# One transformer block on one core: Up's block products 512 wide with partial sums kept in one PSUM bank, and two of four weight sums added in DRAM by transfers during the input projection

## The chip, the core and the metric

The kernel runs on one core of one Trainium2 chip. Its engines, as the profile names them, are PE (matrix products), PEld (PE's weight loads), DVE, ACT and POOL (elementwise work), and SP, which here only issues transfers. All transfers, from whichever engine they are issued, go through the core's 16 DMA engines. Partial sums of products lie in PSUM, in banks of 128 x 512 float32; everything else that is worked on lies in SBUF; weights and intermediates that don't fit lie in DRAM.

The metric is the device time of one execution in microseconds, as the median of several runs. Times inside an execution come from one profiled execution, counted from the start of its span.

## The reference

One layer over 512 tokens of width 2048, in float32:

```python
xn = _rmsnorm(h, norm_mix[l]); y = xn @ w_in[l]
o_gdn = _gdn_group(y[..., :GDN_COLS], ...)      # 8 heads x 128
o_rwkv = _rwkv_group(y[..., GDN_COLS:], ...)    # 16 heads x 64
h = h + concat([o_gdn, o_rwkv]) @ w_out[l]
h = h + _cross_attention(_rmsnorm(h, ...), _rmsnorm(mem, ...), ...)   # 256 memory tokens
hn = _rmsnorm(h, norm_mlp[l])
h = h + jnp.square(jax.nn.relu(hn @ mlp_w_up[l])) @ mlp_w_down[l]     # hidden width 8192
return _rmsnorm(h, norm_final)
```

The line that the change rewrites is `hn @ mlp_w_up`, called Up: 512 x 2048 by 2048 x 8192.

## The kernel before

**Precision.** Each float32 operand of a large product is split into two parts, hi (rounded to a type that PE reads at full rate) and lo (what is left). `split` (L128) does it with one cast on ACT (L130) and one subtraction on DVE (L131). A product is hi x hi + hi x lo + lo x hi, three matmuls through `mm` (L121, L122) into one PSUM bank.

**Stages.** In order of time: the input projection (instructions named py) together with the recurrent heads, up to about 943 us; the projections kp, kq, vp, vo for the cross attention; op (the product with w_out), sc and at (the attention itself); Up from 1688 to 2336 us; Down (dn) from 2336 to 3044 us; the final norm.

**The projection stage** is recorded as chains of instructions and put in order by a list scheduler (`issue` L243, `run` L275), so all its instructions carry the line L247. It keeps a model clock for each engine and issues the chain whose next instruction can start first, with a rank to settle ties. `projections` (L523) is the chain of the large products; one chain each does a group of RWKV heads and a GDN head. Each of these inverts small triangular matrices in `inverse_blocks` (L717): the blocks go to DRAM (nd), come back in another layout (sr or sgi), POOL works through 30 small operations on them, and the result goes out again (bg16T, bg16U, bg8T, bg8U) and comes back to SBUF as r and E (RWKV) or gk and gqn (GDN), from where PE's matmuls ri and gi use it. All these transfers are issued by SP, in program order.

**Up** (L1406 to L1549) is a Strassen scheme in Winograd's form. The hidden columns are 32 blocks of 256; for each block p the 2048 x 256 weights are four quarters a11, a12, a21, a22, each laid out as 128 x 1024 (8 slices of 128 x 128), and the activations four halves of tokens and rows. Seven products, B11, T1, T2, T3, T4, B22 and B21, take the place of eight. Their activation sides are made once, by `place` (L1393) and `put` (L1385), into `comb[i][k]`: a tile of 128 x 512 whose half HA is hi and whose half HB is lo, for each product i and each of 8 slices k. Their weight sides are four sums per block (s1, s2, a21, s4), added on DVE (L1438). `product` (L1421) splits its weights and issues 24 matmuls of 256 columns, here the first 16:

```python
for z, k in enumerate(ks):
    sl = slice(z * P, z * P + P)
    mm(pt, hi[:, sl], comb[i][k][:, HA], start=z == 0, stop=False)
    mm(pt, hi[:, sl], comb[i][k][:, HB], start=False, stop=False)
```

and then 8 of lo with HA, all into the first 256 columns of one bank. Each product has a bank of its own until it is read: the copy of B11 to SBUF on ACT (L1456), and seven additions of 256 columns on DVE that put the four result quarters together (c11, c12 in c1, c21, c22 in c2). `square` (L1535) then applies the norm's scale and the squared ReLU in pieces of 256 columns (DVE L1537, ACT L1538) and stores the block to DRAM (Ud, from ACT, L1540). Block 0 uses another order of products, with B21 and T4 right behind B11, since the norm's scale rstd is made meanwhile (`used`, L1542).

**Buffers and queues.** Weights come in by SP, 512 KB each, four for each block, into three buffers of the tag wraw (NWR) and three of wraw2; split parts have two buffers each (NWS). PSUM tags mx, mg and mm have two banks each. An engine works through its instructions in order, and a semaphore wait holds up all that is queued behind it.

Of the kernel before, what the change touches and what calls it, by code (L numbers as in the profile page):

```python
# [73 lines left out]
def build(tc, I, out):  # L74
# [168 lines left out]
    def issue(op):  # L243
        eng, nm, f, a, k, out, ins, slack = op
        t = start(op)
        d = cost(op)
        f(*a, **k)  # L247
        if eng == "SP":
            clock[eng] = t + 330
            size = math.prod(out.shape) * 4  # L250
            state["dma"] = max(state["dma"], t + 330) + size / 300
            t, eng = max(state["dma"] + 700, t + 2900) + slack[1], "DMA"
        else:
            t += d
            clock[eng] = t
        if eng == "PE":
            state["shape"] = None if ins[0].dtype == F32R else (ins[0].partition_size(), ins[0].free_size())
        if eng == "ACT" and len(a) > 2 and a[2] in (AF.Tanh, AF.Ln, AF.Exp):
# [83 lines left out]
    VOd = [pd.tile([P, 8, 512], F32, name=f"vod{i}", tag=f"vod{i}") for i in range(4)]  # L342

# [852 lines left out]

    issue(pieceload(0))
# [18 lines left out]
    chain(projections(), 4)  # L1216
    chain(rwkv(0), 3)
# [167 lines left out]
    def put(i, k, src):  # L1385
        t = comb[i][k]
        S.copy(t[:, HA], src)
        V.tensor_tensor(out=t[:, HB], in0=src, in1=t[:, HA].bitcast(F32), op=ALU.subtract)
# [4 lines left out]
    def place(i, k, e, o):  # L1393
# [6 lines left out]
        elif i == T3:  # L1400
            sub(e[:, HB], o[:, HB], e[:, HB])
        elif i == T4:
            sub(e[:, HA], e[:, HA], o[:, HA])
        put(i, k, o[:, HB] if i == B22 else o[:, HA] if i == B21 else e[:, HB] if i == T3 else e[:, HA])

    def strassen(nm, pool, src, ks, done, used=None, first=False):  # L1406
# [4 lines left out]
        w = len(ks) * P  # L1411

        def raw(p_, tag, bufs, i):
            cnt[0] += 1
            r = p_.tile([P, 1024], F32, tag=tag, name=f"{tag}_{cnt[0]}", bufs=bufs)[:, 0:w] \
                if p_ is pw else p_.tile([P, pool[1]], F32, tag=tag, name=f"{tag}_{cnt[0]}", bufs=bufs)[:, 0:w]
            if i is not None:
                nc.sync.dma_start(r, src[i])
            return r

        def product(i, tag, a):  # L1421
            cnt[0] += 1
# [12 lines left out]
            return pt  # L1435

        def add(o, a, b, op=ALU.add):
            V.tensor_tensor(out=o, in0=a, in1=b, op=op)  # L1438
# [17 lines left out]
        S.copy(u1, p1)  # L1456
# [250 lines left out]
```

## Time and profile before

| | us |
|---|---|
| median of 3 runs (3055.92 to 3060.02) | 3057.31 |
| span of the profiled execution | 3053.3 |
| median less span | 4.0 |
| PE busy, of the span | 3022.5 |
| DVE busy | 1916.1 |
| ACT busy | 1355.4 |
| POOL busy | 216.3 |
| bytes moved by the core's transfers | 403.14 MB |

PE is the engine to watch: it is busy for all but 31 us of the span. In the views below, "busy" of an engine counts its instructions' time; an idle time in square brackets stands before an instruction and names what ended it; a row of the chain or of the timeline has the start, the length, the engine, line and operation, then output<-inputs, and xN for N equal instructions run together. A line number is that of the kernel before. The page's window figures list the busy time of PE, PEld, DVE, ACT and POOL with their instruction counts, PE's granted clock, the share of the DMA engines' time and the GB/s moved.

### The profile page before, as it was taken

To read this page: it belongs to the slowest core of one execution; us is meant where nothing else is said; L and a number is where in the kernel's file an instruction comes from. 1 tells how busy PE (TensorE), PEld (TensorE's weight loads), DVE (VectorE), ACT (ScalarE), POOL (GpSimd) and SP (SyncE) were. 2 spreads that over 40 slices of the span, in tenths; PEclk is the share of its full clock that TensorE was granted. 3 is DMA by queue.
4 is the path that set the end of the run, shared out by engine and by line. 5 is a ranking of instruction groups with operands and counts; after the bars stand their busy time and mean duration, and the time that the engine had idled before them with its cause. 6 is when DMAs were issued, how large, how long until landed. Compare 5 with 4: busy or idle time off the path is not lost.

```text
span 3053.3 us, 50831 instructions
## 1 busy us (share of the span) xinstructions
PE 3022.5 (99%) x20740; PEld 2607.5 (85%) x20740; DVE 1916.1 (63%) x2881; ACT 1355.4 (44%) x1864; POOL 216.3 (7%) x547
## 2 busy tenths in 40 slices
PE   9999999999999999999999999999999999999998
PEld 7888878878878898778878999999999888888887
DVE  7666666666677647534348888888887443444457
ACT  6455455455555555533336544444444222222234
POOL 0312311312312000000000000000000000000000
PEclk9999999999999999999999999999999999999999
DMA  5322322323425586753323433333334332333335
GB/s 186 104 80 80 108 80 80 108 80 87 135 73 162 172 272 231 262 201 122 110 92 90 142 130 130 132 132 135 125 135 163 124 118 104 125 125 125 113 130 180
DMA packets 226746, 403.14 MB, mean 132 GB/s; under 512 B 91656, under 2 KB 115468, under 8 KB 226512
## 3 DMA queue, kind: packets, MB, share of 16 engines
q1 hardware_dynamic: 210384, 372.62, 37.5%
q10 hardware_dynamic: 16128, 27.27, 2.4%
q8 instruction: 163, 2.67, 0.3%
q14 instruction: 71, 0.58, 0.1%
HBM read 352.23 MB, written 47.59 MB: 131 GB/s over the span
## 4 chain that ended last, share of the span: by engine, by line
PE 95%; DVE 1%; ACT 1%; DMA 1%; issue 1%; POOL 0%; SPq 0%; DVEq 0%; ACTq 0%; POOLq 0%
PE dn L122 23%; PE up L122 21%; PE py L247 21%; PE op L122 6%; PE vp L122 3%; PE sc L122 3%; PE at L122 3%; PE kq L247 3%; PE vo L122 3%; PE kp L247 2%; PE rs L247 1%; PE gs L247 1%; PE pgB L247 1%; PE po L247 0%; PE gpo L247 0%
## 5 line engine op out<-in xcount | busy, mean ns | idle before, releaser
L130 ACT CAST whi<-wraw 128x1024 fp32r<-128x1024 f32 x384 | 403.6, 1051 | 814.3 <-PE dn L122 474.8
L131 DVE TENSOR_TENSOR wlo<-wraw,whi 128x1024 fp32r<-128x1024 f32 x384 | 469.7, 1223 | 135.6 <-ACT whi L130 131.5
L122 PE MATMUL up<-cb,whi 128*128 128x256 f32 x3584 | 467.4, 283 | 1.3 <-ACT whi L130 0.7
L122 PEld LDWEIGHTS up<-cb,whi 128*128 128x128 f32 x3584 | 446.3, 192 | 2.4 <-ACT whi L130 1.7
L122 PE MATMUL dn<-ul,whi 128*128 128x512 f32 (+1 forms) x1032 | 395.0, 389 | 0.9 <-ACT whi L130 0.9
L122 PE MATMUL dn<-uh,whi 128*128 128x512 f32 x1024 | 393.8, 390 | 0.0
L122 PE MATMUL dn<-uh,wlo 128*128 128x512 f32 (+1 forms) x1024 | 384.5, 375 | 0.0
L247 PE MATMUL py<-xhi,whi 128*128 128x512 f32 x928 | 371.8, 401 | 6.1 <-ACT xhi L247 6.0
L247 PE MATMUL py<-xhi,wlo 128*128 128x512 f32 x928 | 371.7, 401 | 0.0
L247 PE MATMUL py<-xlo,whi 128*128 128x512 f32 x928 | 371.4, 400 | 0.3 <-DVE xlo L247 0.3
L247 DVE TENSOR_TENSOR wlo<-wraw,whi 128x1024 fp32r<-128x1024 f32 (+1 forms) x180 | 221.7, 1231 | 128.2 <-ACT whi L247 126.5
L1559 DVE TENSOR_TENSOR h<-h,dn 128x512 f32<-128x512 f32 x112 | 77.0, 688 | 331.1 <-PE dn L122 331.1
L247 ACT CAST whi<-wraw 128x1024 fp32r<-128x1024 f32 (+1 forms) x180 | 188.2, 1046 | 203.0 <-PE py L247 165.3
L122 PE MATMUL up<-cb,wlo 128*128 128x256 f32 x1792 | 251.5, 283 | 0.0
L122 PEld LDWEIGHTS up<-cb,wlo 128*128 128x128 f32 x1792 | 231.2, 192 | 0.0
L122 PEld LDWEIGHTS dn<-ul,whi 128*128 128x128 f32 x1032 | 193.9, 188 | 41.2 <-ACT whi L130 1.2
L122 PEld LDWEIGHTS dn<-uh,whi 128*128 128x128 f32 x1024 | 192.2, 188 | 40.9
L122 PEld LDWEIGHTS dn<-uh,wlo 128*128 128x128 f32 x1024 | 192.3, 188 | 35.0
L247 PEld LDWEIGHTS py<-xhi,whi 128*128 128x128 f32 x928 | 174.9, 188 | 41.2 <-ACT xhi L247 6.2
L247 PEld LDWEIGHTS py<-xlo,whi 128*128 128x128 f32 x928 | 174.9, 188 | 35.6 <-DVE xlo L247 1.4
L247 PEld LDWEIGHTS py<-xhi,wlo 128*128 128x128 f32 x928 | 174.9, 189 | 35.3 <-issue 1.0
L130 ACT CAST whi<-ws 128x1024 fp32r<-128x1024 f32 x96 | 100.5, 1047 | 150.8 <-PE up L122 93.9
(741 smaller groups left out, 5145.4 us busy)
## 6 DMA issues: line engine op xcount, KB each, us to landing
wraw<-in_w_dn SPq DMA_DIRECT2D x144, 512.0 KB, 3.5
wraw<-in_w_up SPq DMA_DIRECT2D x128, 512.0 KB, 3.5
wraw<-in_w_in SPq DMA_DIRECT2D x116, 512.0 KB, 3.6
wraw<-in_wk SPq DMA_DIRECT2D x32, 512.0 KB, 3.9
wraw<-in_wqT SPq DMA_DIRECT2D x32, 512.0 KB, 5.4
wraw<-in_wv SPq DMA_DIRECT2D x32, 512.0 KB, 4.6
wraw<-in_wo SPq DMA_DIRECT2D x32, 512.0 KB, 5.9
wraw<-in_w_out SPq DMA_DIRECT2D x32, 512.0 KB, 3.9
```

Source lines behind the costliest of these rows:

```text
L122: PE.matmul(o, l, r, start=start, stop=stop)
L130: S.copy(hi, src)
L131: V.tensor_tensor(out=lo, in0=src, in1=hi.bitcast(F32), op=ALU.subtract)
L247: f(*a, **k)
L1559: V.tensor_tensor(out=hres[n], in0=hres[n], in1=pt, op=ALU.add)
```

## The change

Three things are changed.

**Wider products.** In `product`, hi meets the whole tile `comb[i][k]`, HA and HB at once: one matmul of 512 columns into a whole bank instead of two of 256 into one half of it. The bank's first half then holds hi x hi (to which 8 matmuls of lo x hi are added), its second half hi x lo. A product is 16 matmuls. Whoever reads a product adds the two halves: `both` copies the second half on ACT and adds the first on DVE; other readers add twice on DVE.

**Accumulating products.** The seven products use three banks, x, y and z. B11, T2, T3 and T4 go one after the other into x, without clearing it, T1 and B22 into y, B21 into z; the running sum is read out in between. So the sums of results are made partly by PE's accumulation. Every block has the order B11, T1, T2, B21, T3, B22, T4. Some signs are turned (B11 and B22 negated, and with them c1's, so that `square` takes the minimum there), and `square` works at the full width of 512.

**Two sums in DRAM.** Of the four weight sums, a21 + a22 and a11 + a21 are made ahead of Up by a new chain, `background`, in the projection stage: at each third step of py, ACT issues two copies of 1 MB from w_up to new arrays in DRAM, and POOL, one step later, two transfers that add another 1 MB of w_up onto them. There are 17 such steps, 32 copies and 32 accumulating transfers. Up then loads the finished sums: five loads of 512 KB for each block instead of four, into three buffers of one kind and five of the other. Two sums stay on DVE. The weights' layout pairs two blocks, so that a row of 8 KB holds both.

```diff
-        d = cost(op)
+        move = nm == "dma_start" and eng != "SP"
+        d = 100.0 if move else cost(op)
...
+    def background():
+
+        for u in range(17):
+            yield after("py", 3 * u + 4)
+            if u < 16:
+                for i, b in ((0, 2), (1, 0)):
+                    yield AC.dma_start(SUMS[i][u], I["w_up"][u, b])
+            if u > 0:
+                for i in (0, 1):
+                    yield GS.dma_start(SUMS[i][u - 1], I["w_up"][u - 1, 1], accum_op=ALU.add, max_dma_last_dim=2048)
...
-    def put(i, k, src):
+    def put(i, k, src, neg=False):
         t = comb[i][k]
-        S.copy(t[:, HA], src)
-        V.tensor_tensor(out=t[:, HB], in0=src, in1=t[:, HA].bitcast(F32), op=ALU.subtract)
+        split(src, t[:, HA], t[:, HB], -1.0 if neg else None)
 
     def sub(o, a, b):
         V.tensor_tensor(out=o, in0=a, in1=b, op=ALU.subtract)
@@ -1398,95 +1414,73 @@
         elif i == T2:
             sub(e[:, HA], o[:, HB], e[:, HA])
         elif i == T3:
-            sub(e[:, HB], o[:, HB], e[:, HB])
+            sub(e[:, HB], e[:, HB], o[:, HB])
         elif i == T4:
-            sub(e[:, HA], e[:, HA], o[:, HA])
-        put(i, k, o[:, HB] if i == B22 else o[:, HA] if i == B21 else e[:, HB] if i == T3 else e[:, HA])
-
-    def strassen(nm, pool, src, ks, done, used=None, first=False):
-
-
-
-
-        w = len(ks) * P
-
-        def raw(p_, tag, bufs, i):
+            sub(e[:, HA], o[:, HA], e[:, HA])
+        put(i, k, o[:, HB] if i == B22 else o[:, HA] if i == B21 else e[:, HB] if i == T3 else e[:, HA],
+            i in (B11, B22))
...
+        def raw(src):
+            i = nraw[0] % 8
+            nraw[0] += 1
+            r = pw.tile([P, 1024], F32, tag="wraw", name=f"ua{nraw[0]}", bufs=NWR) if i % 3 == 0 else \
+                pool.tile([P, 1024], F32, tag="wraw2", name=f"ub{nraw[0]}", bufs=5)
+            nc.sync.dma_start(r, src[:, p % 2 * 1024:p % 2 * 1024 + 1024])
+            return r
+
+        def product(i, pt, a, start=True):
             cnt[0] += 1
-            r = p_.tile([P, 1024], F32, tag=tag, name=f"{tag}_{cnt[0]}", bufs=bufs)[:, 0:w] \
-                if p_ is pw else p_.tile([P, pool[1]], F32, tag=tag, name=f"{tag}_{cnt[0]}", bufs=bufs)[:, 0:w]
-            if i is not None:
-                nc.sync.dma_start(r, src[i])
-            return r
-
-        def product(i, tag, a):
-            cnt[0] += 1
-            hi = pw.tile([P, 1024], F32R, tag="whi", name=f"whi{cnt[0]}", bufs=NWS)[:, 0:w]
-            lo = pw.tile([P, 1024], F32R, tag="wlo", name=f"wlo{cnt[0]}", bufs=NWS)[:, 0:w]
+            hi = pw.tile([P, 1024], F32R, tag="whi", name=f"whi{cnt[0]}", bufs=NWS)
+            lo = pw.tile([P, 1024], F32R, tag="wlo", name=f"wlo{cnt[0]}", bufs=NWS)
             split(a, hi, lo)
-            pt = psb(f"{nm}_{i}", tag)[:, 0:M]
-            for z, k in enumerate(ks):
-                sl = slice(z * P, z * P + P)
-                mm(pt, hi[:, sl], comb[i][k][:, HA], start=z == 0, stop=False)
-                mm(pt, hi[:, sl], comb[i][k][:, HB], start=False, stop=False)
-            for z, k in enumerate(ks):
-                mm(pt, lo[:, z * P:z * P + P], comb[i][k][:, HA], start=False, stop=z == len(ks) - 1)
+            for k in range(8):
+                PE.matmul(pt, hi[:, k * P:k * P + P], comb[i][k], start=start and k == 0, stop=False, skip_group_check=True)
+            for k in range(8):
+                PE.matmul(pt[:, HA], lo[:, k * P:k * P + P], comb[i][k][:, HA], start=False, stop=k == 7, skip_group_check=True)
             if used:
                 used(i)
-            return pt
-
-        def add(o, a, b, op=ALU.add):
+
+        def tt(o, a, b, op=ALU.add):
             V.tensor_tensor(out=o, in0=a, in1=b, op=op)
 
-        def wraw2(i):
-            return raw(pool[0], "wraw2", 3, i)
-
-        def ws():
-            return raw(pool[0], "ws", 2, None)
-
-        a11 = raw(pw, "wraw", NWR, 0)
-        if first:
-            a12, a22 = raw(pw, "wraw", NWR, 3), raw(pw, "wraw", NWR, 2)
-            a21 = wraw2(1)
-        else:
-            a21 = raw(pw, "wraw", NWR, 1)
-            a22, a12 = wraw2(2), wraw2(3)
-        p1 = product(B11, "mx", a11)
-        c1 = sl2()
-        c11, c12 = u1, u4 = c1[:, HA], c1[:, HB]
-        S.copy(u1, p1)
-        if first:
-            p2 = product(B21, "mg", a12)
-            p4 = product(T4, "mx", a22)
-        s1 = ws()
-        add(s1, a21, a22)
-        p5 = product(T1, "mg", s1)
-        s2 = ws()
-        add(s2, s1, a11, ALU.subtract)
-        p6 = product(T2, "mm", s2)
-        c2 = sl2()
-        c21, c22 = u3, u2 = c2[:, HA], c2[:, HB]
-        add(u2, u1, p6)
-        if first:
-            add(c11, u1, p2)
-        add(u4, u2, p5)
-        add(a21, a11, a21, ALU.subtract)
-        p7 = product(T3, "mm", a21)
-        add(u3, u2, p7)
-        add(c22, u3, p5)
-        done(1, HB, c2)
-        if not first:
-            p4 = product(T4, "mx", a22)
-        add(c21, u3, p4, ALU.subtract)
-        done(1, HA, c2)
-        s4 = ws()
-        add(s4, a12, s2, ALU.subtract)
-        p3 = product(B22, "mg", s4)
-        add(c12, u4, p3)
-        done(0, HB, c1)
-        if not first:
-            p2 = product(B21, "mm", a12)
-            add(c11, u1, p2)
-        done(0, HA, c1)
+        def both(o, pt):
+            S.copy(o, pt[:, HB])
+            tt(o, o, pt[:, HA])
+
+        w = [I["w_up"][p // 2, i] for i in range(4)]
+        a11, s1, a12, s3, a22 = (raw(x) for x in (w[0], SUMS[0][p // 2], w[3], SUMS[1][p // 2], w[2]))
+        x, y, z = (psb(f"up{n}{p}", t) for n, t in (("x", "mx"), ("y", "mg"), ("z", "mm")))
+        c1, c2 = sl2(), sl2()
+        u = sl2()
+
+        product(B11, x, a11)
+        both(c1[:, HA], x)
+        product(T1, y, s1)
+        both(u[:, HA], y)
+        tt(s1, s1, a11)
+        product(T2, x, s1, False)
+        both(c1[:, HB], x)
+        product(B21, z, a12)
+        tt(c1[:, HA], c1[:, HA], z[:, HA], ALU.subtract)
+        tt(c1[:, HA], c1[:, HA], z[:, HB], ALU.subtract)
+        product(T3, x, s3, False)
+        tt(c2[:, HB], u[:, HA], x[:, HA])
+        tt(c2[:, HB], c2[:, HB], x[:, HB])
+        tt(a12, a12, s1)
+        product(B22, y, a12, False)
+        tt(c1[:, HB], c1[:, HB], y[:, HA])
+        tt(c1[:, HB], c1[:, HB], y[:, HB])
+        done(0, c1, ALU.min)
+        product(T4, x, a22, False)
+        both(c2[:, HA], x)
+        done(1, c2, ALU.max)
...
-        def square(i, half, c):
-            t = c[:, half]
-            V.scalar_tensor_tensor(out=t, in0=t, scalar=0.0, in1=rstd[:, half], op0=ALU.max, op1=ALU.mult)
-            S.activation(t, t, AF.Square)
-            if half is HA:
-                nc.scalar.dma_start(Ud[p][:, i, :], c)
+        def square(i, c, op):
+            V.scalar_tensor_tensor(out=c, in0=c, scalar=0.0, in1=rstd, op0=op, op1=ALU.mult)
+            S.activation(c, c, AF.Square)
+            nc.scalar.dma_start(Ud[p][:, i, :], c)
```

The following rows are instructions in program order, without times: line, operation, output<-inputs and shape. First PE, a product B11 of a block in the middle of Up (up_0 is the bank of that product, cb_k the slices of `comb`). Before, its last rows for hi and the first for lo:

```order
L122 MATMUL up_0_17130<-cb_5_15817,whi_17126 128x256 x2
L122 MATMUL up_0_17130<-cb_6_15818,whi_17126 128x256 x2
L122 MATMUL up_0_17130<-cb_7_16572,whi_17126 128x256 x2
L122 MATMUL up_0_17130<-cb_0_15812,wlo_17127 128x256
L122 MATMUL up_0_17130<-cb_1_15813,wlo_17127 128x256
L122 MATMUL up_0_17130<-cb_2_15814,wlo_17127 128x256
```

After, the same rows (upx is bank x):

```order
L1444 MATMUL upx_16926<-cb_5_15913,whi_16932 128x512
L1444 MATMUL upx_16926<-cb_6_15914,whi_16932 128x512
L1444 MATMUL upx_16926<-cb_7_16668,whi_16932 128x512
L1446 MATMUL upx_16926<-cb_0_15908,wlo_16933 128x256
L1446 MATMUL upx_16926<-cb_1_15909,wlo_16933 128x256
L1446 MATMUL upx_16926<-cb_2_15910,wlo_16933 128x256
```

Each pair of 256-wide matmuls with hi, shown as x2, has become one of 512 columns; those with lo are as they were.

Second POOL in the projection stage, at the end of an inverse of a GDN head (sgi) and the beginning of the next RWKV group's (sr). Before:

```order
L247 TENSOR_TENSOR sgj_3754<-sgi_3753 32x15
L247 TENSOR_TENSOR sgi_3753<-sgi_3753,sgj_3754 32x15
L247 COPY sgi_3753<-sgi_3753 32x256
L247 MEMSET sr_4610 64x256
L247 MEMSET sr_4610 64x16
L247 TENSOR_TENSOR sr_4611<-sr_4610 64x15
```

After (ws_6 is a sum array in DRAM):

```order
L248 TENSOR_TENSOR sgj_3812<-sgi_3811 32x15
L248 TENSOR_TENSOR sgi_3811<-sgi_3811,sgj_3812 32x15
L248 COPY sgi_3811<-sgi_3811 32x256
L248 DMA ws_6_126<-in_w_up 512x512
L248 DMA ws_6_142<-in_w_up 512x512
L248 MEMSET sr_4672 64x256
L248 MEMSET sr_4672 64x16
L248 TENSOR_TENSOR sr_4673<-sr_4672 64x15
```

Two accumulating transfers now stand between the last operation of one inverse and the first of the next; the two stores and four loads of sgi's result stand on SP at this place, unchanged.

Third ACT in Up's first block, around the making of rstd. Before (whi_16741 is the hi part of T1's weights, whi_16772 of T2's; cb_7 are the last slices of `comb`):

```order
L130 CAST whi_16741<-ws_16739 128x1024
L1387 CAST cb_7_16576<-sl_16535 128x256
L1387 CAST cb_7_16575<-sl_16535 128x256
L1387 CAST cb_7_16577<-sl_16579 128x256
L125 ACT_TABLE_LOAD
L125 ACTIVATE rstd<-pss_16706,cb_e_76 128x512
L126 ACT_TABLE_LOAD
L126 ACTIVATE rstd<-rstd 128x512
L130 CAST whi_16772<-ws_16770 128x1024
```

After (upx and upy are the banks x and y; whi_16772 is T1's, whi_16795 T2's):

```order
L1454 COPY sl_16747<-upx_16744 128x256
L130 CAST whi_16772<-ub_16736 128x1024
L125 ACT_TABLE_LOAD
L125 ACTIVATE rstd<-pss_16837,cb_e_76 128x512
L130 CAST cb_7_16672<-sl_16631 128x256
L126 ACT_TABLE_LOAD
L126 ACTIVATE rstd<-rstd 128x512
L1454 COPY sl_16749<-upy_16745 128x256
L130 CAST whi_16795<-ub_16736 128x1024
```

Before, the casts for the first four products of the block (B11, B21, T4 and T1) stand ahead of the two table loads with rstd; now those for the first two (B11 and T1) do, with the copy of B11's half between them, and the copy of T1's half and the cast for T2, the third product, stand behind.

More of the change, by code (lines that the diff above doesn't have):

```diff
@@ L255, in issue @@
             clock[eng] = t
+            if move:
+                t, eng = t + 15000.0, "DMA"
         if eng == "PE":
             state["shape"] = None if ins[0].dtype == F32R else (ins[0].partition_size(), ins[0].free_size())
-        if eng == "ACT" and len(a) > 2 and a[2] in (AF.Tanh, AF.Ln, AF.Exp):
+        if op[0] == "ACT" and not move and len(a) > 2 and a[2] in (AF.Tanh, AF.Ln, AF.Exp):
             state["table"] = "l" if a[2] == AF.Ln else "e"
@@ L342, in build @@
     VOd = [pd.tile([P, 8, 512], F32, name=f"vod{i}", tag=f"vod{i}") for i in range(4)]
+    SUMS = {i: [pd.tile([P, 2048], F32, name=f"ws{i}_{u}", tag=f"ws{i}_{u}") for u in range(16)] for i in (0, 1)}
     rstd = pc.tile([P, T], F32, name="rstd")
@@ L1216, in build @@
     chain(projections(), 4)
+    chain(background(), 5)
     chain(rwkv(0), 3)
@@ L1506, in build @@
         elif n % 2 == 1:
-            for i in range(2, 7) if n < KD - 2 else (B11, T1, B21, T2, T4, T3, B22):
+            for i in range(2, 7) if n < KD - 2 else (B11, T1, T2, B21, T3, B22, T4):
                 place(i, n // 2, ge, g)
@@ L1549, in used @@
                     usplit(f)
-        strassen(f"up{p}", (pu, 1024), [I["w_up"][p, i] for i in range(4)], list(range(8)), square, used, p == 0)
+        strassen(p, pu, square, used)
     for e in range(7):
@@ L1683, in blocks7 @@
         t = [v[:, k, :, :, m].transpose(2, 1, 0, 3) for m, k in ((0, 0), (1, 0), (1, 1), (0, 1))]
-        return np.ascontiguousarray(np.stack(t, 1).reshape(w.shape[1] // 256, 4, P, -1))
+        t = np.stack(t, 1).reshape(w.shape[1] // 512, 2, 4, P, -1)
+        return np.ascontiguousarray(t.transpose(0, 2, 3, 1, 4).reshape(w.shape[1] // 512, 4, P, -1))
     d["w_up"] = blocks7(a["mlp_w_up"][0])
```

4 lines of the change are left out of this document (3 added, 1 removed).

## The prediction

> **What bounds the kernel now.** I read the page's engine totals and its chain of work first, then the chain in order of time, the windows by stage, and PE's waits.
>
> ```profile
> span 3053.3 us, 50831 instructions
> PE 3022.5 (99%) x20740; PEld 2607.5 (85%) x20740; DVE 1916.1 (63%) x2881; ACT 1355.4 (44%) x1864; POOL 216.3 (7%) x547
> PE 95%; DVE 1%; ACT 1%; DMA 1%; issue 1%; POOL 0%; SPq 0%; DVEq 0%; ACTq 0%; POOLq 0%
> PE dn L122 23%; PE up L122 21%; PE py L247 21%; PE op L122 6%; PE vp L122 3%; PE sc L122 3%; PE at L122 3%; PE kq L247 3%; PE vo L122 3%; PE kp L247 2%; PE rs L247 1%; PE gs L247 1%; PE pgB L247 1%; PE po L247 0%; PE gpo L247 0%
> ```
>
> PE is busy 3022.5 of 3053.3 us, and the chain that ended last is 95% PE. A saving must take time off PE's own instructions; any new wait of PE is paid in full.
>
> In the windows below the columns are the stretch and its length, then busy time of PE, PEld, DVE, ACT and POOL, PE's granted clock, DMA share and GB/s. The stretches are the start, the input projections with the recurrent heads, a stage that leans on transfers (vo), and all but the beginning of Up.
>
> ```profile
> 0.00:12.00 12.00, 5.66 (x13) 3.24 (x13) 6.01 (x19) 6.82 (x11) 2.43 (x11) 1.00 0.76 254
> 12.00:943.00 931.00, 927.65 (x7925) 746.95 (x7925) 627.16 (x1097) 496.63 (x683) 199.99 (x505) 1.00 0.35 101
> 1239.00:1330.00 91.00, 90.50 (x383) 70.20 (x382) 40.84 (x36) 51.18 (x66) 0.00 (x0) 1.00 0.80 270
> 1708.30:2336.50 628.20, 628.20 (x5234) 628.16 (x5235) 524.97 (x696) 283.73 (x382) 0.00 (x0) 1.00 0.38 132
> ```
>
> Up has no idle PE: 628.20 of 628.20 us, at a clock of 1.00. DVE, at 524.97 us, is 84% busy there and behind PE, so the two weight sums that leave DVE are worth nothing by themselves. Up can only get shorter through shorter products.
>
> **Up's products: -24.0 us.** The chain has two unbroken runs of PE, one of 512-wide products (op) and one of Up's 256-wide ones; columns are start, length, instructions.
>
> ```profile
> 1330.56 174.08 PE op L122 x768
> 1708.29 628.07 PE up L122 x5232
> ```
>
> One 512-wide matmul takes 174.08 / 768 = 226.67 ns, one 256-wide 628.07 / 5232 = 120.04 ns. Before, a product is 8 x 3 matmuls of 256: 2.881 us. After, it is 8 of 512 and 8 of 256: 1.813 + 0.960 = 2.774 us. Each of the 7 x 8 x 32 = 1792 merged pairs saves 2 x 120.04 - 226.67 = 13.41 ns, which is **24.0 us**. A block falls from 20.17 to 19.42 us. That op's price holds here is likely: the same operand types, a full bank, the same line.
>
> The Trainium skill speaks against this size. "TensorE: Matmul & The Clock Gate", section "Wait — 56ns, not 53.3ns?", puts the fixed cost of a matmul at about 2.5 ns over its columns (215.7 ns for 512). By it the merge would be worth 1792 x 2.5 = 4.5 us, an estimate. The two rows above disagree: twice 120.04 less 226.67 leaves 13.4 ns for each instruction, and I go by them.
>
> **Can DVE and ACT follow?** Partial sums now stay in a bank that the next product of the same chain adds to, so readers must be done before it starts. The durations (page, and the groups of Up by shape):
>
> ```profile
> L130 ACT CAST whi<-wraw 128x1024 fp32r<-128x1024 f32 x384 | 403.6, 1051 | 814.3 <-PE dn L122 474.8
> L131 DVE TENSOR_TENSOR wlo<-wraw,whi 128x1024 fp32r<-128x1024 f32 x384 | 469.7, 1223 | 135.6 <-ACT whi L130 131.5
> L1438 DVE TENSOR_TENSOR sl<-sl,up 128x256 f32<-128x256 f32 x224 | 93.5, 418 | 99.1 <-PE up L122 99.1
> L1438 DVE TENSOR_TENSOR ws<-wraw,wraw 128x1024 f32<-128x1024 f32 x32 | 39.2, 1224 | 1.4 <-DVE wlo L131 0.4
> L1456 ACT COPY sl<-up 128x256 f32<-128x256 f32 x32 | 11.3, 353 | 0.7 <-ACT sl L1538 0.4 <-DVE acc L1300 0.3
> L1496 DVE TENSOR_TENSOR h<-h,at 128x512 f32<-128x512 f32 x16 | 11.0, 685 | 6.4 <-PE at L122 6.2
> ```
>
> Per block DVE has 7 lo parts and 2 weight sums at 1.22 us, 10 adds at 0.42 and 2 full-width operations at 0.69 (the h row's, the nearest of that size): 16.6 us of 19.42, against 7 x 1.22 + 4 x 1.22 + 7 x 0.42 + 4 x 0.42 = 18.0 of 20.17 before. ACT stays near half. Totals fit; what counts is bank x, freed for T2, T3 and T4 within one foreign product each.
>
> ```profile
> 1990.60 1.60 PE L122 MATMUL up<-cb,whi 128*128 128x256 f32 x12
> 1990.80 0.42 DVE L1438 TENSOR_TENSOR sl<-sl,up 128x256 f32<-128x256 f32 x1 [0.60 <-PE up L122]
> ```
>
> A reader starts 0.20 us after the next product's first matmul. Laying out the new order with products at 0, 2.77, 5.55, 8.32, 11.10, 13.87, 16.64 us: B11 ends at 2.77, ACT's copy 2.97 to 3.32, DVE's add to 3.75, or 4.2 behind a lo part; T2 needs x at 5.55. After T2 (8.32) the same pair ends at about 10.3, T3 needs 11.10. After T3 (13.87) two adds on DVE with a lo part between them end at about 16.1, T4 needs 16.64. Slacks of 1.3, 0.8 and 0.5 us: hidden, with the third place the tightest. I cost it at 0.
>
> **Up's first block: +1.8 us.** It starts while the norm before it still finishes on ACT.
>
> ```profile
> 1688.24 2.08 PE L122 MATMUL up<-cb,whi 128*128 128x256 f32 x16
> 1696.82 1.28 ACT L125 ACT_TABLE_LOAD   x1
> 1698.12 0.69 ACT L125 ACTIVATE rstd<-pss,cb_e 128x512 f32<-128x512 f32 x1
> 1698.82 1.28 ACT L126 ACT_TABLE_LOAD   x1
> 1700.12 0.63 ACT L126 ACTIVATE rstd<-rstd 128x512 f32<-128x512 f32 x1
> ```
>
> At 1708.29, 144 of the first block's 168 matmuls are done: 20.05 us for 17.29 of work, 2.8 lost. After, ACT's order is the copy of B11's half, the cast for T1, then both table loads with rstd, the copy of T1's half, and the cast for T2. T1 waits for the copy and a cast behind B11's end: 0.20 + 0.35 + 1.05 + about 0.15 = 1.75 us. From that cast's end ACT runs 1.28 + 0.69 + 0.35 + 1.28 + 0.63 + 0.35 + 1.05 = 5.63 us before T2 can start, while T1 lasts 2.77: 2.86 late. Together 4.6 instead of 2.8, **+1.8**. Bounds: 0 if the casts come earlier, +5 if the special order was worth more.
>
> **Background sums: +5 us.** 32 copies and 32 accumulating transfers of 1 MB go from DRAM to DRAM. Laid beside the trace by their neighbours in the order, the first copies are issued behind ACT's first row below, two more behind the second; most accumulates stand behind POOL's last copy of an inverse, the last ones behind the row at 838.57.
>
> ```profile
> 73.93 0.62 ACT L247 CAST sumh_pn<-sr 128x512 fp32r<-128x512 f32 x1
> 143.44 1.03 ACT L247 CAST whi<-wraw 128x1024 fp32r<-128x1024 f32 x1
> 379.44 1.06 POOL L247 COPY sgi<-sgi 32x256 f32<-32x256 f32 x1
> 421.01 0.50 POOL L247 MEMSET sr<- 64x256 f32 x2 [40.52 <-DVE AR L247]
> 838.57 0.62 POOL L247 COPY sgi<-sgi 32x256 f32<-32x256 f32 x1
> ```
>
> Issuing is the small part. ACT pays 32 x 0.33 us (its store, next fence), 11 us, on an engine busy 497 of 931 us. No row shows POOL issuing a transfer; by SP's dearest issue row, 0.59, it is 1.2 us a pair, by nothing at all 0, and POOL has 40.52 us free behind its copy. I take 0; the cover would be gone if a pair took over 40 us.
>
> The traffic is the larger part. 67 MB at 254 / 0.76 = 334 GB/s for a full share take 200 us if each byte counts once, 400 if read and written count; between 74 and 840 us that lifts the share of 0.35 to 0.61 or 0.87. At 0.80, in vo, PE lost 0.50 us in 91.
>
> ```profile
> 1971.12 0.33 ACTq L1540 DMA_DIRECT2D ud<-sl  x1
> wraw<-in_w_in SPq DMA_DIRECT2D x116, 512.0 KB, 3.6
> wraw<-in_wo SPq DMA_DIRECT2D x32, 512.0 KB, 5.9
> E<-bg16U SPq DMA_DIRECT2D x32, 64.0 KB, 3.3
> gk<-bg8T SPq DMA_DIRECT2D x16, 64.0 KB, 4.0
> ```
>
> vo's load (in_wo) landed in 5.9 us, the projections' in 3.6: about 2 us more for each transfer. The weights' loads are issued far ahead; what is short is the heads' chain through DRAM, E and gk, loaded shortly before PE needs them. Head 2, then head 0, then PE's one wait for such a load:
>
> ```profile
> 367.20 0.59 SPq L247 DMA_DIRECT2D E<-bg16U  x1
> 377.06 0.27 PE L247 MATMUL ri2s<-k,E 64*64 64x64 f32 x2
> 382.47 0.58 SPq L247 DMA_DIRECT2D gk<-bg8T  x1
> 392.34 0.68 PE L247 MATMUL gi2x<-gk,gEs 64*64 64x64 f32 x16
> 148.05 0.58 SPq L247 DMA_DIRECT2D E<-bg16U  x1
> 149.25 0.27 PE L247 MATMUL ri0t<-k,E 64*64 64x64 f32 x1
> PE ri0t L247 <- DMA E<-bg16U: 0.9, 1, 0.9
> ```
>
> E has 9.9 us for a landing of 3.3, gk 9.9 for 4.0: 5 to 6 us of slack. Head 0 has none, and two copies come 4 us before its E: 2 MB at 334 GB/s is 6.3 us of backlog, of which I take 3 to 4 as PE's wait, and 1 to 2 for all other heads. Bounds: 0 (all hidden) and rival B.
>
> A queue of its own could shield the small loads; "DMA: Bandwidth & Descriptors" in the Trainium skill, section "Issuing engines are not separate DMA queues", says that transfers from any engine run on the same 16 DMA engines and interleave. By that rule the price stands; no trace so far shows it across issuing engines.
>
> **Sum.** -24.0 + 1.8 + 5 = -17.2. The profiled execution is 3053.3 of span; the median of runs is 4.0 above it, kept as constant: 3057.3 - 17.2 = **3040.1 us**.
>
> **Rivals.**
> (B) *The background transfers delay the small DRAM round trips beyond their slack.* A head's chain has four of them in a row (store, read back, store, load), and a burst is issued right between its stores and loads. At +2 us each that is 8 against 5 to 6 of slack; 64 KB pieces ahead of small ones could make it more. It decides from 22.2 / 16 = 1.4 us beyond slack in each of 16 recurrent chains. At 3 to 5 us each: +48 to +80, **3083 to 3115, slower**. For it: the positions, and head 0's wait. Against: bursts are over in 6 to 13 us, and vo hardly suffered.
> (C) *Bank x is read too late.* If readers end 0.3 us late at all three places, 32 x 3 x 0.3 = 29 us eat the saving: 3057.3 + 4.8 = **3062**; the third place alone, 0.3 late, gives 3050. Against: DVE has 2.8 us free in a block.
> (D) *Merging buys nothing*, because 512 columns of these operands cost two 256-wide products: 3057.3 + 6.8 = **3064**. Against: op's row.
> (E) *Only the skill's 2.5 ns is saved*: as a mechanism, a fixed part of 2.5 ns and the rest columns: 3057.3 - 4.5 + 6.8 = **3060**. Against: the two durations in the chain.
>
> **How the numbers follow.** Forecast 0.60 (3033 to 3051), B 0.24, C 0.08, D 0.05, E 0.03. To hold 8 in 10 the range goes from 3033 (nothing lost, -24.0) over C to E up to B's lowest end, 3085; the forecast's own range is 3033 to 3051. A measurement of this kernel can tell about 0.2%, 6.1 us: faster is below 3051.2, slower above 3063.4. Faster: 0.58 (nearly all of the forecast). Same: 0.02 + 0.05 of C + 0.04 of B + 0.02 of D + 0.03 of E = 0.16. Slower: 0.20 of B, 0.03 of C, 0.03 of D = 0.26.
>
> **What the profile after would show.** Up's steady run at 226.7 and 120 ns, 19.42 us a block, with no PE wait on DVE's or ACT's reads of x. The first block ends about 1.8 us later relative to its work. In 12 to 943 us PE's idle time grows from 3.4 to about 8 us, at head 0, at a DMA share of 0.6 to 0.87. I am wrong if PE's waits there list E, gk, gqn or r at most heads (B), if PE in Up waits for L1438's successors (C), or if 512-wide products take 238 (E) to 240 ns (D).

## The result, and the profile after

The changed kernel takes 3201.56 us (median of 4, 3198.13 to 3207.24) against 3058.66 for the kernel before (4 runs): a ratio of 1.0469 [1.0454, 1.0484]. It is **4.7% slower**, 143 us, where 17 us less was forecast. The page's totals and its row of PE's granted clock:

```profile
span 3196.3 us, 47565 instructions
PE 3056.2 (96%) x18948; PEld 2545.8 (80%) x18948; DVE 1879.2 (59%) x2849; ACT 1369.3 (43%) x1896; POOL 239.1 (7%) x579
PEclk9989989899899999999999999999999999999999
```

PE has 140 us without work where it had 31, and for the first time its clock is not full in every slice. Where this lies is read from the first matmul of kq, the stage behind the recurrent heads. PE's rows of that group (durations least, median, most in ns; start of the first and last), before and after:

```profile
L247 PE MATMUL kq<-khi,whi x256: 277/283/290, 1052.6 to 1145.5; 128*128 128x256 f32 x128
```

```profile
L248 PE MATMUL kq<-khi,whi x256: 277/283/283, 1210.8 to 1302.9; 128*128 128x256 f32 x128
```

| stretch, from PE's first matmuls | before | after | difference |
|---|---|---|---|
| start to kq | 1052.6 | 1210.8 | +158.2 |
| kq to Up | 635.6 | 634.5 | -1.1 |
| Up | 648.0 | 633.9 | -14.1 |
| Down and the end | 717.1 | 717.1 | 0.0 |

So the change has two separate results: Up is 14 us shorter, and the projection stage, in which nothing but the background transfers was added, is 158 us longer (2.6 of these also without the transfers, by e1 below). PE's largest waits after, in us in all, times, and longest:

```profile
PE pW L248 <- DMA lw<-in_w2a: 33.5, 5, 17.5
PE pqk L248 <- DVE gqn L248: 22.7, 4, 8.0
PE ri0t L248 <- DMA E<-bg16U: 14.8, 1, 14.8
PE gi5x L248 <- DMA gk<-bg8T: 12.8, 2, 9.0
PE gn L248 <- DVE suml_gn L248: 7.0, 3, 3.4
PE gi1x L248 <- DMA gk<-bg8T: 6.9, 2, 5.5
```

Four of the six wait for a small load of a head's chain; pqk and gn wait for DVE's part of a head's norm. The landings, to be held against 3.3 for E and 4.0 for gk before (lw was 4.5):

```profile
ws<-in_w_up POOLq DMA_DIRECT2D x32, 1024.0 KB, 15.7
E<-bg16U SPq DMA_DIRECT2D x32, 64.0 KB, 6.6
gk<-bg8T SPq DMA_DIRECT2D x16, 64.0 KB, 12.0
gqn<-bg8U SPq DMA_DIRECT2D x16, 64.0 KB, 12.5
lw<-in_w2a SPq DMA_DIRECT2D x8, 64.0 KB, 13.1
```

One place shows how it comes about. POOL, SP and PE around 578 us, from three answers of the timeline:

```profile
577.62 0.60 POOL L248 COPY sgi<-sgi 32x256 f32<-32x256 f32 x1
578.17 4.14 POOL L248 DMA_DIRECT2D ws<-in_w_up  x4
...
579.41 0.59 SPq L248 DMA_DIRECT2D gk<-bg8T  x1
...
582.45 0.61 SPq L248 DMA_DIRECT2D lw<-in_w2a  x1
...
599.19 2.04 PE L248 MATMUL pW<-wa,lw 64*128 64x512 f32 x2 [11.14 <-DMA lw<-in_w2a]
...
606.24 0.63 PE L248 MATMUL py<-xhi,whi 128*128 128x512 f32 x1
```

```profile
594.00:599.00 5.00, 0.00 (x0) 0.00 (x0) 0.00 (x0) 0.00 (x0) 0.00 (x0) 0.50 1.13 204
602.60:606.00 3.40, 3.40 (x12) 1.78 (x12) 2.32 (x5) 0.68 (x2) 0.00 (x0) 0.50 1.11 231
```

The inverse's last copy ends, and four adding transfers of 1 MB start at once; one to five microseconds behind them SP issues gk, gqn and lw. The DMA share is at its full (the figure goes a little over 1) while the adds run. lw lands over 16 us after its issue, PE idles 11.14 us, and in that idle time its granted clock falls to 0.50 and stays there beyond 606: a py matmul takes 0.63 us, 0.39 at full clock. That is why the stage lost more than PE waited. PE's idle time ahead of kq, summed over the trace, went from 11.3 to 118.0 us, which is 106.7 of the 158.2; the other 51.5 us are slower matmuls. The clock records bear this out: PE worked for 106 us of that stretch at half clock, and half of that, 53 us, is lost.

### The profile page after: what moved, and what is told of

It reads as the page before. It is cut to its first block, busy times and chain, and to the rows that moved or that the text cites. A ratio compares the mean times of both kernels' runs of the same rounds, so it can differ in the third digit from the quotient of the medians.

```text
span 3196.3 us, 47565 instructions
## 1 busy us (share of the span) xinstructions
PE 3056.2 (96%) x18948; PEld 2545.8 (80%) x18948; DVE 1879.2 (59%) x2849; ACT 1369.3 (43%) x1896; POOL 239.1 (7%) x579
## 5 line engine op out<-in xcount | busy, mean ns | idle before, releaser
L130 ACT CAST whi<-wraw 128x1024 fp32r<-128x1024 f32 x256 | 269.3, 1052 | 631.6 <-PE dn L122 463.0
L131 DVE TENSOR_TENSOR wlo<-wraw,whi 128x1024 fp32r<-128x1024 f32 x256 | 313.5, 1225 | 133.9 <-ACT whi L130 130.0
L248 PE MATMUL py<-xhi,whi 128*128 128x512 f32 x928 | 378.3, 408 | 6.8 <-ACT xhi L248 6.8
L248 PE MATMUL py<-xhi,wlo 128*128 128x512 f32 x928 | 378.7, 408 | 0.4 <-DVE wlo L248 0.4
L248 PE MATMUL py<-xlo,whi 128*128 128x512 f32 x928 | 377.9, 407 | 0.3 <-DVE xlo L248 0.3
L1444 PE MATMUL upx<-cb,whi 128*128 128x512 f32 x1024 | 257.1, 393 | 4.0 <-ACT whi L130 2.4
L130 ACT CAST whi<-ub 128x1024 fp32r<-128x1024 f32 x140 | 147.0, 1051 | 159.1 <-PE upx L1444 81.0
L1444 PEld LDWEIGHTS upx<-cb,whi 128*128 128x128 f32 x1024 | 184.4, 189 | 37.4 <-ACT whi L130 2.6
L131 DVE TENSOR_TENSOR wlo<-ub,whi 128x1024 fp32r<-128x1024 f32 x140 | 171.1, 1222 | 22.3 <-ACT whi L130 19.9
L1446 PEld LDWEIGHTS upx<-cb,wlo 128*128 128x128 f32 x1024 | 140.5, 191 | 10.1
```

Of the source, the lines that this page charges most:

```text
L130: S.copy(hi, src)
L131: V.tensor_tensor(out=lo, in0=src, in1=hi.bitcast(F32), op=ALU.subtract)
L1444: PE.matmul(pt, hi[:, k * P:k * P + P], comb[i][k], start=start and k == 0, stop=False, skip_group_check=True)
L1446: PE.matmul(pt[:, HA], lo[:, k * P:k * P + P], comb[i][k][:, HA], start=False, stop=k == 7, skip_group_check=True)
```

## The experiments

Times are medians; for e2 to e6 and e10 it is the time of a single run, and as the ten runs of e9 and of e12 lie 18 and 25 us apart, small differences between single runs count for little. The kernel before, on the same chip, had a median between 3056.3 and 3057.2 in each set. "kq" is the start of that stage, "idle" PE's idle time ahead of it, "gk" the median landing.

| run | us | kq | idle | gk | Up |
|---|---|---|---|---|---|
| changed kernel | 3201.6 | 1210.8 | 118.0 | 12.0 | 633.9 |
| e1 no transfers | 3042.0 | 1055.2 | 13.0 | 4.1 | 632.0 |
| e2 copies on POOL | 3236.1 | 1246.1 | 141.0 | 12.6 | 633.8 |
| e3 copies alone, on ACT, 64 KB pieces | 3061.1 | 1074.9 | 23.7 | 4.0 | 632.1 |
| e4 POOL's alone, not adding, 4 KB | 3110.0 | 1123.0 | 52.1 | 11.2 | 633.1 |
| e5 as e4, 64 KB | 3104.2 | 1118.2 | 52.4 | 9.4 | 633.3 |
| e6 as e3, 2 KB | 3091.1 | 1103.8 | 36.7 | 4.0 | 633.1 |
| e7 all at the program's front | 3230.8 | 1243.5 | 181.2 | 3.8 | 633.3 |
| e8 sums by POOL in SBUF | 3177.9 | 1055.8 | 14.2 | 4.1 | 769.8 |
| e9 all in op, at and Up | 3052.0 | 1054.2 | 12.2 | 3.7 | 643.3 |
| e10 copies, and POOL's not adding | 3153.5 | 1163.5 | 89.9 | 13.2 | 632.8 |
| e11 four sums on DVE | 3046.3 | 1056.9 | 12.9 | 4.0 | 637.2 |
| e12 adds held back | 3065.9 | 1080.2 | 28.0 | 3.9 | 632.1 |

**The two parts apart, and the first suspect.** The trace offered a second explanation. Five times ACT stands at the second of its two copies until a transfer of SP's has landed, and the two rows take 9.9 to 11.8 us together (the expectation of e2 has six times and 11.4). I took this for a completion semaphore that the two share; the trace shows only what ended the hold. First a hold that ended when bg8T was stored, then one that ended with a weight's load, with what followed on DVE and PE:

```profile
144.77 11.45 ACTq L248 DMA_DIRECT2D ws<-in_w_up  x2
156.27 0.63 ACT L248 ACTIVATE sg<-y 128x512 f32<-128x512 f32 x1 [11.37 <-DMA bg8T<-sgi]
...
272.85 11.56 ACTq L248 DMA_DIRECT2D ws<-in_w_up  x2
284.50 1.28 ACT L248 ACT_TABLE_LOAD   x1 [11.04 <-DMA wraw<-in_w_in]
...
289.48 0.69 DVE L248 TENSOR_TENSOR gqn<-gq,sg 128x512 f32<-128x512 f32 x1 [0.81 <-ACT sg L248]
...
290.32 2.04 PE L248 MATMUL pqk<-gqn,gkn 128*128 128x128 f32 x8 [7.82 <-DVE gqn L248]
```

Theory A was that PE is late by these holds, theory B that the traffic makes the small loads late. Four runs, each with one edit:

```diff
e1
-    chain(background(), 5)
-        ... (w[0], SUMS[0][p // 2], w[3], SUMS[1][p // 2], w[2])
+        ... (w[0], w[1], w[3], w[1], w[2])
e2
-                    yield AC.dma_start(SUMS[i][u], I["w_up"][u, b])
+                    yield GS.dma_start(SUMS[i][u], I["w_up"][u, b])
e3
-                    yield GS.dma_start(SUMS[i][u - 1], ...)
e4
-                    yield AC.dma_start(SUMS[i][u], I["w_up"][u, b])
-                    ... I["w_up"][u - 1, 1], accum_op=ALU.add, max_dma_last_dim=2048)
+                    ... I["w_up"][u - 1, 1], max_dma_last_dim=2048)
```

> The changed kernel without its background chain; Up loads the quarters a21 in place of the two sums (so its sums are other sums, of the same size), all else as changed. All theories: the projection stage is back at the time of before (kq begins at 1052 us, 1211 in the changed kernel), Up keeps what the trace of the changed kernel shows for it, 634.1 us against 648.1. So 3057 - 14 = 3043 us, and the whole loss of 157 us lies in the background transfers. If Up's new form cost the stages around it something, it would stay above 3050.

> The 32 copies are issued by POOL, in front of the accumulates, in place of ACT; ACT issues no transfer in the projections any more. Theory A (ACT stands at its copies for completion semaphores that it shares with SP, six times about 11.4 us, and PE is late by that): the holds go, the time falls by 50 to 90 us, to 3110 to 3150. Theory B (the traffic itself, above all POOL's, makes the heads' small loads late, and ACT's holds lie beside PE's waits): it stays within 25 us of 3201.

> The 32 accumulating transfers are left out, the copies on ACT stay (the arrays hold one quarter in place of a sum). Theory A: ACT's holds stay, and so does most of the loss: over 3120 us. Theory B: what is left is short bursts in large pieces; the small loads land in 4 to 6 us instead of 12, PE's waits shrink to under 30 us: 3050 to 3085.

> The copies on ACT are left out, and POOL's 32 transfers write without adding (the arrays hold one quarter in place of a sum): the same places, pieces of 2 KB, half the bytes. Theory B in the form that POOL's transfers as such delay what SP issues: over 3110 us. In the form that it is the adding that makes them long (15.7 us to landing): under 3080, with a landing of 8 us or less. Theory A: about 3045 to 3060, since ACT holds no copy.

e1 came to 3041.98, ratio 0.9959 [0.9945, 0.9973]: Up alone is worth 14 us, and the whole loss is the transfers'. e2 took ACT's holds away and got slower by 34 us. Its wait for pqk and its landing of lw:

```profile
PE pqk L248 <- DVE gqn L248: 4.8, 2, 3.0
lw<-in_w2a SPq DMA_DIRECT2D x8, 64.0 KB, 21.0
```

The holds did cost something: two of them stand ahead of PE's waits for pqk of 7.8 and 8.0 us, and pqk's 22.7 us fell to 4.8. But the copies now stood at POOL's places, and lw landed in 21.0 us instead of 13.1. e2 therefore doesn't price the holds by themselves. e3 lost 19 us against e1; e4, with the same bytes from POOL, no adding and no copy on ACT, 68. So **theory A falls as the main cause**. Its holds end with late landings of SP's transfers, and with ACT's copies alone, in e3, the longest is 6 us. e4's landings:

```profile
ws<-in_w_up POOLq DMA_DIRECT2D x32, 1024.0 KB, 9.6
gk<-bg8T SPq DMA_DIRECT2D x16, 64.0 KB, 11.2
```

That is neither form of B as I had put it (over 3110 or under 3080): adding isn't needed to make gk late, but it is not all.

**Place or piece.** e3 and e4 differ in the place of issue and in the size of their pieces. e5 and e6 cross the two, though not exactly: in the DMA records the small pieces are packets of 4 KB in e4 and of 2 KB in e6.

```diff
e5, from e4
-                    ... I["w_up"][u - 1, 1], max_dma_last_dim=2048)
+                    ... I["w_up"][u - 1, 1])
e6, from e3
-                    yield AC.dma_start(SUMS[i][u], I["w_up"][u, b])
+                    yield AC.dma_start(SUMS[i][u], I["w_up"][u, b], max_dma_last_dim=2048)
```

> As the run with POOL's 32 transfers alone that don't add (3110 us), at the same places, but in pieces of 64 KB in place of 4 KB; the arrays hold one quarter in place of a sum. If the number of pieces is what stops the small loads: like the copies on ACT, 3050 to 3075 us, gk landing in under 6 us. If the place is what matters (right behind an inverse, ahead of its loads): 3095 to 3120, gk landing in 9 us or more.

> As the run with the copies on ACT alone (3061 us), at the same places, but in pieces of at most 4 KB in place of 64 KB; the arrays hold one quarter in place of a sum. If the number of pieces matters: over 3085 us. If the place matters: 3050 to 3070.

Loss against e1, in us: ACT's places 19 (large pieces) and 49 (small), POOL's places 62 and 68. At POOL's places gk lands late whatever the pieces, at ACT's it lands in 4.0 whatever the pieces. The place counts first; small pieces cost 30 us more at ACT's places, and 6 at POOL's, which single runs can't tell from nothing. Up to here, the place and the engine that issues are changed together; e12 below, whose adds also come from POOL, separates them.

**What the adding costs.** e10 is the changed kernel with POOL's transfers not adding (the edit of e4's last two lines alone).

> The changed kernel, but POOL's 32 transfers write without adding (same places and bytes from the source, pieces of 4 KB; the arrays hold one quarter in place of a sum). If copies and POOL's transfers only add up: 3042 + 19 + 68 = 3129 us, and the remaining 72 us of the changed kernel are the adding's, whose packets of 2 KB take 176 ns against 84 of a plain one. If it is the two together that are late: 3180 to 3205, and the adding itself costs next to nothing.

3153: 24 us over the sum of the two parts, 48 under the changed kernel. Both expectations were too simple: as far as single runs show it, parts that are late together cost more than their sum, and the adding has a price of its own. In the traces' records an adding packet of 2 KB takes 176 ns (median), one of e6's plain copies of 2 KB 84, and the plain 4 KB packets that stand in their place in e10 159.

**The same transfers elsewhere.** e7 and e9 issue all 64 from POOL behind results of op, at and Up, by this function; e7 has only the first line and the two transfers, e9 the store ahead of the copy as well:

```diff
+    def pace(t):
+        nc.gpsimd.tensor_copy(pacer, t[:, 0:1])
+        nc.gpsimd.dma_start(d[:, 0:1], pacer)
+        nc.gpsimd.dma_start(d, I["w_up"][h // 2, (2, 0)[h % 2]])
+        nc.gpsimd.dma_start(..., I["w_up"][(h - 1) // 2, 1], accum_op=ALU.add, max_dma_last_dim=2048)
```

> All 64 transfers, the copies too, are issued by POOL in later stages: one copy and one accumulate behind each second product of op (8 times), each fourth of at (4 times) and each of Up's first 21 blocks, each waiting on POOL for a result of that stage. The result is the reference's. Theory B (it is the heads' round trips through DRAM that the transfers make late, and not traffic as such): no PE wait is left in the projections, Up's loads have 20 us and more to spare: 3040 to 3050 us, as without the transfers. If traffic as such slows PE's stages: over 3060.

> As the run in which the transfers were moved behind op's and at's products and Up's blocks, but each copy is now held there by a store of 128 x 1 values from the stage's result into its array ahead of it (in that run nothing held the copies, and all 64 transfers went to the front of the program). The result is the reference's. Theory B (what costs time is that the heads' round trips through DRAM come late, not traffic as such): no wait of PE in the projections, kq begins at 1055 us, Up's loads have 20 us and more to spare: 3040 to 3050 us, faster than before. If traffic as such slows PE's stages, wherever it runs: over 3060.

e7 missed its aim. Nothing tied its transfers to the small copy ahead of them, so the program's order had them all at its front; the DMA share is full for 320 us, PE waits up to 119.4 us for a weight, and the time is 3230.8. e9 ran as meant: 3052.04, ratio 0.9989 [0.9975, 1.0003]. The projections are undisturbed, and the price is 11 us in Up, against e1. Its window over Up, and a wait of PE's and one of ACT's there:

```profile
1700.00:2300.00 600.00, 593.19 (x3372) 520.00 (x3373) 465.83 (x633) 286.19 (x393) 53.47 (x82) 1.00 0.80 232
```

```profile
PE upx L1461 <- DVE sl L1468: 8.2, 9, 1.7
ACT sl L1471 <- POOL pacer L1326: 22.3, 10, 3.7
```

PE's wait is for DVE's readers of bank x. These wait in part for ACT's copies, and ACT in turn waits until POOL's small copy has read the result buffer that is to be used again. So at least a part of the 11 us is the price of this way of holding the transfers, not of the traffic. A DMA share of 0.80 in Up goes with 11 us at most, one of 0.58 in the projections with 156.

**The same transfers in the projections, a few microseconds later.** e12 keeps copies and adds in the projections, and PE's order, but holds the adds until the small loads that stood behind them have landed:

```diff
+    def held():
+        for j in range(8):
+            yield GS.tensor_copy(pacer, loaded[2 * j + 1][:, 0, 0:1])
+            if j < 7:
+                yield GS.tensor_copy(pacer, lws[j + 1][:, 0:1])
+            for u in (2 * j, 2 * j + 1):
+                for i in (0, 1):
+                    yield GS.dma_start(SUMS[i][u], I["w_up"][u, 1], accum_op=ALU.add, max_dma_last_dim=2048)
```

> The changed kernel with the same 32 copies on ACT and the same 32 adding transfers on POOL, in the projections, but POOL issues the adds of a head, four at a time, only when that head's gqn and the next head's lw have landed (POOL copies one column of each ahead of them). The result is the reference's and PE's order is that of the changed kernel. Theory B in the form that the place decides (the adds stand right ahead of loads that PE needs soon): gk, gqn and lw land in about 4 us again, what is left is the copies' 19 us and a little, 3060 to 3085 us. In the form that the adds' time on the DMA engines counts wherever it lies in the projections (they fill 16 engines for about 6 us each): over 3130.

3065.85 (3057.09 to 3082.31, 10 runs), ratio 1.0034 [1.0015, 1.0054]: 136 us less than the changed kernel, with all bytes still moved. The window of the projections (of the changed kernel, then of e12) and e12's landings:

```profile
12.00:943.00 931.00, 829.79 (x6765) 659.34 (x6765) 530.47 (x921) 411.55 (x566) 186.12 (x450) 0.92 0.58 149
```

```profile
12.00:943.00 931.00, 914.18 (x7810) 733.26 (x7809) 612.49 (x1067) 478.55 (x654) 223.41 (x535) 0.99 0.62 163
```

```profile
ws<-in_w_up POOLq DMA_DIRECT2D x32, 1024.0 KB, 18.2
gk<-bg8T SPq DMA_DIRECT2D x16, 64.0 KB, 3.9
lw<-in_w2a SPq DMA_DIRECT2D x8, 64.0 KB, 3.8
```

The DMA share is higher than in the changed kernel, the adds take longer to land, and PE is busy 84 us more in the same stretch. Against e3, the copies alone, the adds now cost about 5 us (kq at 1080.2 and 1074.9).

**Up without transfers.** Were they needed? e8 adds the two sums on POOL in SBUF, e11 on DVE, there behind the first two products:

```diff
-        a11, s1, a12, s3, a22 = (raw(x) for x in (w[0], SUMS[0][p // 2], w[3], SUMS[1][p // 2], w[2]))
+        a11, a22, s3, a12 = (raw(x) for x in (w[0], w[2], w[1], w[3]))
+        s1 = pool.tile([P, 1024], F32, tag="ws", name=f"us{p}", bufs=2)
+        nc.gpsimd.tensor_tensor(out=s1, in0=s3, in1=a22, op=ALU.add)      # e8; V in e11
+        nc.gpsimd.tensor_tensor(out=s3, in0=a11, in1=s3, op=ALU.add)      # e8; V in e11
```

> No transfers: the two sums of each block are added by POOL in SBUF during Up from the loaded quarters (four loads a block as before). The result is the reference's. By POOL's 1.295 us for 128x512 one sum takes 2.6 us, two 5.2 of 19.6 us a block, so they hide: 3040 to 3048 us. If POOL's adds slow DVE's, which is busy 85% of Up, or come too late for T1: over 3055.

> No transfers: all four weight sums on DVE during Up, as in the kernel before, with the 512-wide products in three banks. The result is the reference's. DVE then has 16.6 + 2 x 1.22 = 19.0 us of work in a block of 19.55. If that fits: 3042 to 3050 us, and the transfers were not needed. If DVE reads bank x late at one to three places in each block by 0.5 to 1 us: 3058 to 3110, and the two sums had to leave DVE.

e8: 3177.89, ratio 1.0391 [1.0374, 1.0408]. POOL's and DVE's groups (busy, mean ns of one), and PE's wait:

```profile
L131 DVE TENSOR_TENSOR wlo<-ua,whi 128x1024 fp32r<-128x1024 f32 x64 | 142.0, 2219 | 1.0 <-ACT whi L130 0.3
L1460 POOL TENSOR_TENSOR ua<-ua,ua 128x1024 f32<-128x1024 f32 x32 | 102.6, 3206 | 2.5
L1450 DVE TENSOR_TENSOR ub<-ub,us 128x1024 f32<-128x1024 f32 x32 | 91.1, 2847 | 0.0
L131 DVE TENSOR_TENSOR wlo<-us,whi 128x1024 fp32r<-128x1024 f32 x64 | 78.4, 1225 | 24.5 <-ACT whi L130 24.5
```

```profile
PE upx L1443 <- DVE sl L1450: 83.6, 32, 3.1
```

DVE's operations of 1.22 us take 2.2 and 2.8 on average where POOL adds beside them: the two hold each other up, bank x is read late once in each block, and PE waits 83.6 us. It is the mechanism of rival C, with another cause. Up is 138 us longer than in e1; of the other 54 us, 51 are lost by PE working at half clock. The clock is 0.93 on the mean although no wait for x is over 3.1 us:

```profile
1692.00:2461.00 769.00, 681.24 (x3584) 587.95 (x3582) 622.85 (x685) 312.82 (x432) 182.47 (x64) 0.93 0.34 112
```

e11, with all four sums on DVE, takes 3046.26, ratio **0.9967 [0.9953, 0.9981]**: 0.3% faster than the kernel before, faster than the changed one too, and without any added traffic. Up is 5 us longer than in e1, mostly in its first block, where T1 waits 4.8 us for its sum's cast:

```profile
PE upy L1443 <- ACT whi L130: 4.8, 1, 4.8
PE upx L1443 <- DVE sl L1450: 1.4, 1, 1.4
```

## Why the prediction was wrong

**The bound** was read rightly: PE sets the time, and each wait is paid. It is paid more than once: the clock that PE loses in a wait was in no term of my sum, and it made a third of the loss. The Trainium skill has the rule in "TensorE: Matmul & The Clock Gate", section "HAM oscillation — how this bites in real kernels": no idle gaps of PE over about 3.4 us. The trace agrees in part: after gaps of 1.3 and 3.3 us, at 429 and 418, py is at full rate within 2 us, after those of 11.1 and 14.8 us, at 588 and 150, only 13.5 and 6.5 us on. But a wait of 2.4 us in Up's first block (rows below) and waits of at most 3.1 us in e8 halved the clock too; here the measurements decide, and waits of 2 to 3 us are not safe.

**Up's products, -24.0**: right mechanism, too large. Two rows of the chain, one block apart:

```profile
1996.99 1.84 PE upz L1444 x8
...
2016.54 1.84 PE upz L1444 x8
```

A block takes 19.55 us, a product 2.793, not 2.774. The eight wide matmuls take 1.84 us, 230 ns each, where op's row gave 226.67. That leaves (2.881 - 2.793) x 224 = 19.7 us. Why they are 3 ns dearer than op's stays open. The Trainium skill's 2.5 ns for each matmul ("TensorE: Matmul & The Clock Gate", section "Wait — 56ns, not 53.3ns?") would have given 4.5 us, an estimate; the measurement is against it.

**DVE and ACT follow, 0**: right, but for one place. PE waits for a reader of bank x once in all of Up, 1.6 us in the last block, and in e11 1.4 with 2.4 us more work for DVE in a block. (Rival C's 3062 left out the 6.8 us of the other two terms; with them, as in its figure for the third place alone, it is 3069.)

**The first block, +1.8**: right for the waits; the clock came on top. The changed kernel's rows and PE's window figures, then T2 in e1:

```profile
1845.27 1.98 PE L1444 MATMUL upx<-cb,whi 128*128 128x512 f32 x8
...
1850.06 2.14 PE L1444 MATMUL upy<-cb,whi 128*128 128x512 f32 x8 [0.56 <-ACT whi L130]
...
1855.50 2.69 PE L1444 MATMUL upx<-cb,whi 128*128 128x512 f32 x8 [2.36 <-ACT whi L130]
...
1857.99 1.91 PE L1446 MATMUL upx<-cb,wlo 128*128 128x256 f32 x8
...
1859.69 2.26 PE L1444 MATMUL upz<-cb,whi 128*128 128x512 f32 x8
```

```profile
1856.80:1859.70 2.90, 2.90 (x13) 2.61 (x12) 2.27 (x2) 1.05 (x1) 0.00 (x0) 0.50 0.05 20
```

```profile
1699.73 2.11 PE L1443 MATMUL upx<-cb,whi 128*128 128x512 f32 x8 [2.38 <-ACT whi L130]
```

T1 starts 2.0 us late (1.75 foreseen) and T2 2.7 more (2.86). T2 then takes 4.2 us: it waits for nothing in between, but from 1856.8 on PE's granted clock is halved. In e1 T2 has the same wait ahead of it, keeps the full clock and takes 2.9 us. So the block loses 4.8 us in e1, where 4.6 were foreseen and 2.8 were lost before, and 6.3 in the changed kernel. The wait in the last block makes that block 1.6 us longer in e1 and 1.9 in the changed kernel, which no term had. In e1 that gives -19.7 + 2.0 + 1.6 = -16.1, and 632.0 - 648.0 = -16.0 was measured; in the changed kernel it gives -19.7 + 3.5 + 1.9 = -14.3, and -14.1 was measured.

**Background sums, +5: this step failed.** It measured 156 (kq at 1210.8, in e1 at 1055.2). The sum took each transfer as 2 us later, from vo's landings, and set that against 5 to 6 us of slack; it gave head 0 a price and all other heads 1 to 2 us together. vo's share of 0.80 is a steady stream of SP's own loads in their order. Here a burst is issued in front of the very loads that PE needs next, and they land when the burst is nearly over: 12 to 13 us instead of 4, beyond any slack in the rows that I had shown. e12 settles it: the same burst, issued when those loads have landed, costs about 5 us over the copies alone. The issue of the copies, put at 11 us of ACT's time that cost PE nothing, also held ACT five times, and PE behind two of these holds. I had the positions, and used them only for a rival. The lw loads, in the end PE's largest wait, I had not looked at.

**Rival B** (0.24, 48 to 80 us) was the right mechanism, and the point from which it decides was passed: 156 / 16 = 9.7 us a chain, 6.6 of it waiting. Its 2 us a transfer was the same borrowed size, and the clock was missing. The result, 3201.6, lies above the range and above B's own end. Rivals C, D and E did not happen in this kernel. The Trainium skill's "DMA: Bandwidth & Descriptors", section "Issuing engines are not separate DMA queues", is borne out: POOL's transfers delayed SP's, gk from 4.0 to 12.0 us.

## What to carry to other kernels

In this kernel a transfer in the background was not priced by its bytes or by the mean DMA share, but by which small load is issued within the next few microseconds behind it, and how soon it is needed: hold the burst until that load has landed. Where PE is the bound, a wait can cost well over its length through PE's clock: 51.5 us on top of 106.7 in the changed kernel, 51 on 84 in e8, and 25 on 24 in e6. Before work is moved off an engine that has little to spare, try whether it still fits: four sums on DVE did, at 3046 us.

## What was not expected of the hardware

After a wait of 11.1 us PE was back at full rate only 13.5 us later, and a wait of 2.4 us could halve the clock (Up's first block in the changed kernel) or leave it (in e1). An adding DRAM transfer moves packets of 2 KB in 176 ns, a plain one (e6) in 84. POOL spends 1.03 us on issuing one such transfer (4.14 for four). An elementwise add on POOL stretches a DVE add of 1.22 us to 2.8 on average (e8). The Trainium skill's "SBUF — State Buffer", section "SBUF: two separate sides", has a port pair that the two share and lock for whole instructions; e8's rows agree with it.
